# Where the block sums of the output weights are made, and how many buffers the block sums of h land in, in an encoder layer on one core

## The chip, the cores and the metric

The kernel runs on one core of one Trainium2 chip. The metric is the device time of one execution in microseconds (us); lower is better. Times before: 1134.73, 1137.67 and 1137.10 us, median 1137.1. The profile comes from a further execution.

The engines named below: TensorE (PE) multiplies matrices and leaves the sums in PSUM, which has eight banks here; VectorE (DVE) and GpSimd (POOL) do elementwise work, ScalarE (ACT) copies and evaluates functions, and SyncE (SP) issues every DMA of this kernel, in one queue and in order. An instruction that waits holds up all that stands behind it on its engine.

## The reference

One encoder layer is applied to two inputs with the same weights: a prompt of 512 tokens and a sample of 1024, each token with 1024 channels. Cut to what matters:

```python
h = rmsnorm(x, norm_g)
qa, ka, va, za, qb, kb, vb, zb, ga, gb = split(h @ w_in)
oa = (neighbourhood_attention(qa, ka, va, rpb_a) * silu(za)) @ w_o_a
ob = (window_gqa_attention(qb, kb, vb, t5_table, sink_b) * silu(zb)) @ w_o_b
merged = sigmoid(ga) * oa + sigmoid(gb) * ob
return x + merged @ w_out
```

All of it is 32-bit arithmetic.

## The kernel before, in words

**Products in three matmuls.** A 32-bit operand is split into a part `hi` that TensorE's fast 32-bit format holds exactly and a rest `lo` (`split`, L1170 on ScalarE for hi, L1175 on VectorE or GpSimd for lo). A product of two operands is then hi x hi, hi x lo and lo x hi (L1288, L1289, L1290). Weights go into `whi` and `wlo`, six buffers each; a chunk of h or of another moving operand is `hh` and `hl`. Each product of a 512x128 weight block with 512 columns is 12 matmuls.

**The stages.** For the prompt: attention, then the dense phase (`dense_phase`) with a z stage (silu gates), a gate stage, the merge (the two output products of the branches times their gates) and the output stage (`merged @ w_out` plus x). Then the same for the sample. In the profile the prompt's output stage lies from 351 to 394 us, the sample's attention from 394 to about 786, its z stage from 786, its output stage from about 1040 to the end.

**Seven products for eight.** The prompt's dense stages use plain products (`pair_classic`, `CLASSIC_P = (4, 8, 4)`): a pair of output chunks takes four raw weight blocks of 128x512, named (chunk m, half j). The sample's dense stages use Strassen's form in Winograd's variant: a pair takes seven products of half the size instead of eight. For it four sums of the raw weight blocks are needed (s1 = (1,0) + (1,1), s2 = s1 - (0,0), s3 = (0,0) - (1,0), s4 = (0,1) - s2), and four block sums of the moving operand, which `stored_sums` loads from DRAM (`t_d` for h, written long before; `m_d` for the merged values), block by block into buffers `U` (four), and splits into tiles `T`. Two of the seven products, and two of the weights, need no sum of h: (0,0) and (1,0) go with blocks of h; so does the seventh, s4 with the block (1,1) of h. The other four products use T.

**The z stage of the sample.** Ahead of the pairs, one product for each pair that needs only h is left in `fr` or `fl` (`kept_z`), and a second is added to it. `pair_strassen` then makes the remaining five products of each pair: three with T into running sums, the fourth with T, and last the one on h with s4.

**The output stage of the sample.** `pairs_apart` works in two rounds over four pairs. The first makes the products that need no T, the second the four others. The first round loads four raw blocks a pair, makes s1 to s4 on VectorE or GpSimd, and stores s1, s2 and s3 to `s_d` in DRAM (L1430); the second round loads them back (L1452) beside one raw block.

**What sets the order.** A planner (`Flow.run`) simulates the engines with costs for each operation and writes out one order for each engine before the kernel is built. Each operation has a priority number, lower first; among the operations that are ready an engine takes the lowest. Buffers of a tag are a ring: those of `IN_TURN` (`raw`, `whi`, `wlo`, `U`, `T`, `S`, `C`, `ot`, `w32`) are taken strictly in turn. A buffer is free when all operations that hold it have ended, DMAs included. `raw` has four buffers (`load_raw`, L1250 to 1253). On the chip the order of each engine is fixed; semaphores carry the real waits.

**Between the prompt and the sample** the pools of the prompt are closed when their last user has ended (`f.stage`), and the sample's mask and bias tables are then loaded. The attention weights (`att_weights`, L600 loads into `w32`, L602 and L607 split) follow the output weights in the same `whi` and `wlo` rings.

## Time and profile before

| what | before |
|---|---|
| median of three runs | 1137.1 us |
| profiled execution, its own time | 1136.88 us |
| its span, first to last instruction | 1135.1 us |
| TensorE busy | 1121.6 us, 99% of the span, 6079 matmuls |
| VectorE, ScalarE, GpSimd busy | 863.8, 653.7, 327.1 us |
| bytes moved by DMA | 186.11 MB, 164 GB/s mean |
| granted TensorE clock | 1.000 |

A row of a timeline gives the start in us from the span's first instruction, the duration in us, engine, line, operation, output tile, inputs, shapes and count; in brackets stands the idle time of that engine just before, and what ended it. Matmuls are pipelined, so their durations overlap: the distance from one start to the next tells the pace. A row of windows gives the stretch, its length, and for each of TensorE's matmuls, TensorE's weight loads, VectorE, ScalarE and GpSimd the busy time and the number of instructions, then the granted clock, the share of the DMA engines and GB/s. A row of the chain of waits gives a start, a duration and what the time went to.

Here is how many matmuls TensorE began in the stretches around the changed places; at full pace with 512 columns a stretch of 20 us has 90:

```profile
780.00:800.00 20.00, 20.00 (x94) 16.55 (x93) 12.30 (x23) 13.04 (x24) 0.00 (x0) 1.00 0.77 229
800.00:820.00 20.00, 19.31 (x82) 14.90 (x81) 16.78 (x28) 10.14 (x19) 0.47 (x1) 1.00 0.93 309
820.00:840.00 20.00, 19.57 (x86) 15.86 (x86) 19.09 (x27) 9.56 (x20) 8.68 (x8) 1.00 0.48 155
840.00:860.00 20.00, 20.00 (x90) 16.56 (x89) 17.36 (x26) 5.59 (x12) 5.93 (x5) 1.00 0.80 242
```

### The profile page before, as it was taken

What the parts mean: (1) busy time and instruction counts of PE and PEld (TensorE: products, weight loads), DVE (VectorE), ACT (ScalarE), POOL (GpSimd) and SP (SyncE); (2) the same over time, 40 slices, a digit from 0 to 9 for tenths busy, and PEclk for the clock granted to TensorE, in tenths of its full rate; (3) what the DMA queues carried; (4) which work ended last, traced back from release to release, by engine and by line L of the source; (5) the groups of instructions that cost most, each with busy time, mean ns of one, the idle gap of its engine ahead of it and who ended that gap; (6) DMA issues with size and microseconds to landing.
All of it is one profiled execution on the core that took longest, in us unless ns stands there. A gap on an engine that the chain in (4) does not pass through costs nothing.

```text
span 1135.1 us, 18686 instructions
## 1 busy us (share of the span) xinstructions
PE 1121.6 (99%) x6079; PEld 973.9 (86%) x6079; DVE 863.8 (76%) x1995; ACT 653.7 (58%) x1498; POOL 327.1 (29%) x432
## 2 busy tenths in 40 slices
PE   8999999999999999999999999999999999999998
PEld 6999988888888889999899988988788888788887
DVE  5888797587765468887868888885888866779874
ACT  6777987644433246574759888876534434522440
POOL 4654433000010044433414344420033221124221
PEclk9999999999999999999999999999999999999999
DMA  7854533488786422121312314244958645868982
GB/s 261 273 157 139 183 115 103 110 262 260 241 276 196 159 91 72 29 79 29 91 32 84 82 38 112 57 131 127 300 187 244 218 167 180 297 219 281 302 279 93
DMA packets 139108, 186.11 MB, mean 164 GB/s; under 512 B 29897, under 2 KB 68561, under 8 KB 139010
## 3 DMA queue, kind: packets, MB, share of 16 engines
q1 hardware_dynamic: 139010, 184.91, 51.4%
q8 instruction: 48, 0.79, 0.3%
q14 instruction: 50, 0.41, 0.1%
HBM read 138.71 MB, written 50.88 MB: 167 GB/s over the span
## 4 chain that ended last, share of the span: by engine, by line
PE 89%; DMA 4%; DVE 4%; ACT 1%; issue 1%; SPq 0%; POOL 0%; DVEq 0%; POOLq 0%; ACTq 0%
PE p L761 25%; PE x L1288 8%; PE x L1290 8%; PE x L1289 8%; PE x L1063 5%; PE x L1026 5%; PE x L934 5%; PE d L1288 4%; PE d L1289 4%; PE d L1290 4%; PE p L1289 4%; PE p L1290 4%; PE p L1288 4%; PE x L861 2%; DMA ot<-u_d 1%
## 5 line engine op out<-in xcount | busy, mean ns | idle before, releaser
L761 PE MATMUL p<-whi,hh 128*128 128x384 f32 x384 | 133.6, 348 | 0.0
L761 PE MATMUL p<-whi,hl 128*128 128x384 f32 x384 | 132.4, 345 | 0.0
L761 PE MATMUL p<-wlo,hh 128*128 128x384 f32 x384 | 132.2, 344 | 0.0
L978 ACT ACTIVATE sb<-sb,mx 128x384 f32<-128x384 f32 (+1 forms) x192 | 107.7, 565 | 22.9 <-DVE mx L969 22.6
L1170 ACT ACTIVATE whi<-raw 128x512 fp32r<-128x512 f32 (+1 forms) x136 | 79.4, 599 | 67.4 <-PE x L1289 46.3
L1289 PE MATMUL x<-T,whi 128*128 128x512 f32 x284 | 110.7, 390 | 0.3 <-DVE T L1175 0.2
L1288 PE MATMUL x<-T,whi 128*128 128x512 f32 x284 | 110.6, 390 | 0.0
L1290 PE MATMUL x<-T,wlo 128*128 128x512 f32 x284 | 110.5, 389 | 0.0
L761 PE MATMUL p<-whi,hb 128*128 128x384 f32 x384 | 107.8, 346 | 0.0
L1037 DVE TENSOR_TENSOR pp<-x,pp 128x512 fp32r<-128x512 f32 (+1 forms) x136 | 82.6, 639 | 20.3 <-ACT pp L1032 19.2
L1175 DVE TENSOR_TENSOR wlo<-raw,whi 128x512 fp32r<-128x512 f32 (+1 forms) x109 | 73.3, 682 | 26.5 <-ACT whi L1170 26.0
L1175 POOL TENSOR_TENSOR wlo<-raw,whi 128x512 fp32r<-128x512 f32 (+1 forms) x27 | 32.1, 1199 | 172.9 <-ACT whi L1170 160.2
L799 POOL TENSOR_TENSOR rs_r<-rs_v,mhalf 128x4 f32<-128x4 f32 (+1 forms) x72 | 79.9, 1109 | 5.7
L1032 ACT ACTIVATE pp<-x 128x512 fp32r<-128x512 f32 (+1 forms) x136 | 70.9, 561 | 18.2 <-PE x L1026 17.1
L792 POOL TENSOR_SCALAR rs_v<-ss 128x4 f32<-128x4 f32 (+1 forms) x72 | 26.0, 361 | 185.1 <-DVE ss L785 181.7
L1063 PE MATMUL x<-pp,v 128*128 128x256 f32 (+1 forms) x368 | 76.6, 322 | 0.0
L1288 PE MATMUL x<-hh,whi 128*128 128x512 f32 x196 | 76.4, 390 | 0.1
L1290 PE MATMUL x<-hh,wlo 128*128 128x512 f32 x196 | 76.3, 389 | 0.0
L1289 PE MATMUL x<-hl,whi 128*128 128x512 f32 x196 | 76.2, 389 | 0.0
L761 PEld LDWEIGHTS p<-whi,hl 128*128 128x128 f32 x384 | 72.8, 190 | 1.3 <-issue 1.0
L761 PEld LDWEIGHTS p<-whi,hh 128*128 128x128 f32 x384 | 73.0, 190 | 1.1 <-issue 0.5
L761 PEld LDWEIGHTS p<-wlo,hh 128*128 128x128 f32 x384 | 72.9, 190 | 0.9 <-issue 0.5
(381 smaller groups left out, 3011.9 us busy)
## 6 DMA issues: line engine op xcount, KB each, us to landing
raw<-in_w_g_dram SPq DMA_DIRECT2D x84, 256.0 KB
w<-in_w_att_dram SPq DMA_DIRECT2D x46, 384.0 KB
raw<-in_w_z_dram SPq DMA_DIRECT2D x40, 256.0 KB
ot<-o_d SPq DMA_DIRECT2D x36, 256.0 KB
raw<-in_w_out_dram SPq DMA_DIRECT2D x36, 256.0 KB
g_d<-C SPq DMA_DIRECT2D x34, 256.0 KB
fr<-in_w_g_dram SPq DMA_DIRECT2D x28, 256.0 KB
out_dram<-C SPq DMA_DIRECT2D x19, 256.0 KB
```

The costliest lines, as they stand in the source:

```text
L761: pe.matmul(ps.t[:, :GW], part[u](k), mv.t[:, c], start=k == 0 and m == 0, stop=k == KC - 1 and m == 2,)
L799: lambda e: nc.gpsimd.tensor_tensor(r.t[:, :nn], rv.t[:, :nn], mhalf[:, :nn], op=ALU.pow),
L934: pe.matmul(pss[2 * pair + i].t[:, :width], q.t[rows, u, at : at + P], kv[:, tiles[0] : tiles[-1] + 1 : step], start=n == 0, stop=n == 2,)
L978: act.activation(sb.t[:, :width], sb.t[:, :width], AF.Exp, bias=mx.t[:, i : i + 1], scale=-1.0, accum_out=sm.t[:, i : i + 1],)
L1032: lambda e, pt=pt, pp=pp, nn=nn: act.activation(pp.t[:, 0, :nn], pt.t[:, :nn], AF.Copy),
L1037: lambda e, pt=pt, pp=pp, nn=nn: dve.tensor_tensor(pp.t[:, 1, :nn], pt.t[:, :nn], pp.t[:, 0, :nn].bitcast(F32), op=ALU.subtract),
L1063: pe.matmul(out(), v.t[:, vs], mv(), start=first, stop=last)
L1170: (("act", ACT_(n)),), lambda e: act.activation(hi(), src(), AF.Copy), prio,
L1175: lambda e: engines[e].tensor_tensor(lo(), src(), hi().bitcast(F32), op=ALU.subtract), prio,
L1288: pe.matmul(out, hi.t[:, cs], mh(), start=first and k == 0, stop=False, **more)
L1289: pe.matmul(out, hi.t[:, cs], ml(), start=False, stop=False, **more)
L1290: pe.matmul(out, lo.t[:, cs], mh(), start=False, stop=last and k == len(ws) - 1, **more)
```

## The change

Three things are changed.

1. In the prompt's output stage `pair_classic` calls the new `weight_sums` for each pair: once both chunks' raw blocks have been split, the four sums are made in place in the raw buffers, one after the other, and all four are stored to `s_d`, which is now one tile for the whole kernel. In the sample's output stage `pairs_apart` makes no sums any more: the first round loads two raw blocks and s4, the second s1, s2, s3 and one raw block as before.
2. `stored_sums` for h lands every second block in `fh` or `w32` (two buffers each) instead of `U`, so that eight blocks can be under way; all these loads wait for the stage's opening.
3. In the first pair of the sample's z stage the product with s4 on h is issued before the products with T, and its PSUM bank is kept until its result is added at the pair's end.

```diff
@@ -403,6 +403,9 @@
     t_d = dpool.tile([4, 4, P, NT_S // 2], F32, tag="t_d", name="t_d")
     o_d = {geo.nt: dpool.tile([2, 8, P, geo.nt], F32, tag=f"o_d{geo.nt}", name=f"o_d{geo.nt}") for geo in (gp, gs)}
 
+    s_d = dpool.tile([4, 4, P, 512], F32, tag="s_d", name="s_d")
+    s_saves = {}
+
     def expand(geo, h, lo):
 
         run = 3 * geo.cw * 16
@@ -1147,7 +1150,6 @@
         g_d = dpool.tile([2, 8, P, nt], F32, tag=f"g_d{nt}", name=f"g_d{nt}")
         p_d = None if short else dpool.tile([2, 4, P, sn], F32, tag="p_d", name="p_d")
         m_d = None if short else dpool.tile([4, 4, P, sn], F32, tag="m_d", name="m_d")
-        s_d = None if short else dpool.tile([8, 3, P, nh], F32, tag="s_d", name="s_d")
         stores = {}
         h_reads = []
         tags = iter(ROTA * 50)
@@ -1228,6 +1230,9 @@
 
             return moving_sums(tv, ops)
 
+        def spare(tag):
+            return f.value(wpool, [P, nh], F32, tag, {"fc": 1}.get(tag, 2))
+
         def stored_sums(prio, d, after):
 
             tv, ops = {}, {}
@@ -1235,13 +1240,13 @@
                 tv[j] = tuple(f.value(tp, [P, 4, nh], F32R, "T", 8) for _ in range(2))
                 vh, vl = tv[j]
                 for k in range(4):
-                    st = tile_("U", 4)
+                    st = spare(("fh", "w32")[k // 2]) if not short and d is t_d and k % 2 else tile_("U", 4)
                     dma(
-                        lambda st=st, j=j, k=k: nc.sync.dma_start(st.t, d[j, k]), 512 * nh, prio, new=[st],
-                        after=after(j, k),
+                        lambda st=st, j=j, k=k: nc.sync.dma_start(st.t[:, :nh], d[j, k]), 512 * nh, prio, new=[st],
+                        after=[*after(j, k), *([opened] if d is t_d else [])],
                     )
                     ops[j, k] = split(
-                        lambda vh=vh, k=k: vh.t[:, k], lambda vl=vl, k=k: vl.t[:, k], lambda st=st: st.t, nh, prio,
+                        lambda vh=vh, k=k: vh.t[:, k], lambda vl=vl, k=k: vl.t[:, k], lambda st=st: st.t[:, :nh], nh, prio,
                         (vh, k == 0), (vl, k == 0), [st],
                     )
             return moving_sums(tv, ops)
@@ -1309,11 +1314,31 @@
 
             return mov
 
-        def pair_classic(srcs, post, prio, mov_h, after=lambda i: ()):
+        def weight_sums(i, raw, ends, prio):
+            o = None
+            for j, out, in0, in1, op in (
+                (2, (1, 1), (1, 0), (1, 1), ALU.add), (1, (1, 0), (0, 0), (1, 0), ALU.subtract),
+                (0, (0, 0), (1, 1), (0, 0), ALU.subtract), (3, (0, 1), (0, 1), (0, 0), ALU.subtract),
+            ):
+                v, a, b = raw[out], raw[in0], raw[in1]
+                o = tt(
+                    lambda v=v: v.t, lambda a=a: a.t, lambda b=b: b.t, op, 512, prio, hold=[v, a, b],
+                    after=[*ends, *([o] if o else [])],
+                )
+                s_saves[i, j] = dma(
+                    lambda v=v, j=j: nc.sync.dma_start(s_d[i, j], v.t), 262144, prio, after=[o], hold=[v],
+                )
+
+        def pair_classic(srcs, post, prio, mov_h, after=lambda i: (), sums_of=None):
 
             i = 0
+            raws, ends = {}, []
             for m, src in enumerate(srcs):
-                ws = weight_tiles([load_raw(src[j], prio - 2) for j in range(2)], 4, prio)
+                raws.update({(m, j): load_raw(src[j], prio - 2) for j in range(2)})
+                ws = weight_tiles([raws[m, j] for j in range(2)], 4, prio)
+                ends += [x for w in ws for *_, ops in w for x in ops]
+                if m and sums_of is not None:
+                    weight_sums(sums_of, raws, ends, prio + 0.5)
                 for n in halves:
                     ps = bank(next(tags))
                     o = product(ps, ws[0], mov_h(0, n), prio, True, False, after(i))
@@ -1368,6 +1393,7 @@
                     (("act", ACT_(sn)),), lambda e: act.activation(p1.t, a.t[:, :sn], AF.Copy), prio, new=[p1], use=[a]
                 )
                 result(0, 0, p1, mul(1, mov_h(1, 0)))
+            ps7 = mul(6, mov_h(1, 1)) if here and not prio else None
             add(u2, p1, mul(2, mov_t(1)))
             add(u3, u2, mul(3, mov_t(2)))
             b = mul(4, mov_t(0))
@@ -1375,7 +1401,7 @@
             result(1, 1, u3, b)
             result(1, 0, u3, mul(5, mov_t(3)), ALU.subtract)
             if not last:
-                result(0, 1, u4, mul(6, mov_h(1, 1)))
+                result(0, 1, u4, ps7 or mul(6, mov_h(1, 1)))
                 return
 
             c = seed(0, sn, sn, u4, prio)
@@ -1395,12 +1421,14 @@
                 post(0, nh + s.start, nh // 2, c, False, prio, s.start, [last_op])
 
 
-        def spare(tag):
-            return f.value(wpool, [P, nh], F32, tag, {"fc": 1}.get(tag, 2))
-
         def pairs_apart(jobs, prio, mov_h, mov_t, late, seed=None, ready=()):
 
             kept = []
+
+            def load_sum(i, j, prio):
+                v = tile_("raw", 4, 512)
+                dma(lambda: nc.sync.dma_start(v.t, s_d[i, j]), 262144, prio - 2, new=[v], after=[s_saves[i, j], start])
+                return v
 
             def take(ps, w, mov, pr, first, last, after=(), again=False, n=sn):
                 o = product(ps, w, mov, pr, first, last, [*after, *ready], n, again)
@@ -1412,24 +1440,9 @@
                     (("act", ACT_(sn, False)),), lambda e: act.activation(out.t, ps.t[:, :sn], AF.Copy), pr, new=[out], use=[ps],
                 )
 
-            for i, (at, srcs, post) in enumerate(jobs):
+            for i, (srcs, post) in enumerate(jobs):
                 pr = prio + i / 8
-                raw = {(m, j): load_raw(srcs[m][j], pr - 2) for m, j in ((0, 0), (1, 0), (1, 1), (0, 1))}
-                s1, s2, s4, s3 = (tile_("S", 3, 512) for _ in range(4))
-                saves = []
-                for j, out, in0, in1, op in (
-                    (2, s1, raw[1, 0], raw[1, 1], ALU.add), (0, s2, s1, raw[0, 0], ALU.subtract),
-                    (None, s4, raw[0, 1], s2, ALU.subtract), (1, s3, raw[0, 0], raw[1, 0], ALU.subtract),
-                ):
-                    tt(
-                        lambda out=out: out.t, lambda in0=in0: in0.t, lambda in1=in1: in1.t, op, 512,
-                        pr - 0.5 + (j == 1), new=[out], use=[in0, in1],
-                    )
-                    if j is not None:
-                        saves.append(dma(
-                            lambda j=j, out=out, at=at: nc.sync.dma_start(s_d[at, j], out.t), 262144, pr, use=[out],
-                        ))
-                w = weight_tiles([raw[0, 0], raw[0, 1], s4], 6, pr - 0.5)
+                w = weight_tiles([load_raw(srcs[0][0], pr - 2), load_raw(srcs[0][1], pr - 2), load_sum(i, 3, pr)], 6, pr - 0.5)
                 p1, c = (spare(t) for t in (("fr", "fl"), ("fr", "fl"), ("fh", "fc"), ("fh", "w32"))[i])
                 ps, p7 = bank(next(tags)), bank(next(tags))
                 take(ps, w[0], mov_h(0, 0), pr, True, True)
@@ -1442,16 +1455,11 @@
                     leave(c, p7, pr)
                 take(ps, w[1], mov_h(1, 0), pr, False, True, [o], True)
                 post(0, 0, sn, ps, True, pr)
-                kept.append((p1, c, saves))
-
-            for i, ((at, srcs, post), (p1, c, saves)) in enumerate(zip(jobs, kept)):
+                kept.append((p1, c))
+
+            for i, ((srcs, post), (p1, c)) in enumerate(zip(jobs, kept)):
                 pr = late + i
-                raw = []
-                for j in range(3):
-                    v = tile_("raw", 4, 512)
-                    dma(lambda v=v, j=j, at=at: nc.sync.dma_start(v.t, s_d[at, j]), 262144, pr - 2, new=[v], after=saves)
-                    raw.append(v)
-                w = weight_tiles([*raw, load_raw(srcs[1][1], pr - 2)], 6, pr - 0.5)
+                w = weight_tiles([*(load_sum(i, j, pr) for j in range(3)), load_raw(srcs[1][1], pr - 2)], 6, pr - 0.5)
                 pv = lambda v: (lambda: v.t[:, :sn])
 
                 def mul(j, t):
@@ -1744,7 +1752,7 @@
         mov_h = blocks(m_ops, nh)
         if not short:
             jobs = [
-                (4 + i, [[w_out[c, j] for j in range(2)] for c in (2 * i, 2 * i + 1)], lambda m, *a, i=i: post_out(2 * i + m, *a))
+                ([[w_out[c, j] for j in range(2)] for c in (2 * i, 2 * i + 1)], lambda m, *a, i=i: post_out(2 * i + m, *a))
                 for i in range(4)
             ]
             seeds = lambda i: lambda m, *a: with_x(2 * i + m, *a)
@@ -1755,7 +1763,7 @@
             srcs = [[w_out[c, j] for j in range(2)] for c in (2 * i, 2 * i + 1)]
             post = lambda m, *a, i=i: post_out(2 * i + m, *a)
             if i < o_classic:
-                pair_classic(srcs, post, 20 + i, mov_h)
+                pair_classic(srcs, post, 20 + i, mov_h, sums_of=i)
             else:
                 seed = lambda m, *a, i=i: with_x(2 * i + m, *a)
                 pair_strassen(srcs, post, 20 + i, mov_h, mov_t, seed, i == 3)
```

## The prediction, made before the change was run

> **What bounds the kernel now.** I read the page's shares first, then the count of matmuls in short windows, then TensorE's own rows where a window holds too few, and last the chain of waits behind each of these places.
>
> ```profile
> PE 1121.6 (99%) x6079; PEld 973.9 (86%) x6079; DVE 863.8 (76%) x1995; ACT 653.7 (58%) x1498; POOL 327.1 (29%) x432
> ```
>
> TensorE is busy for 1121.6 of 1135.1 us, and the change takes no matmul away. So it can only win back places where TensorE's rows stand apart. In the dense stages a 512-column matmul starts 0.227 us after the one before it; what a step has beyond that is lost. In the z stage of the sample (786 to 826 us) the wide steps are these:
>
> ```profile
> 811.13 0.50 PE L1288 MATMUL x<-T,whi 128*128 128x512 f32 x1
> 811.85 0.50 PE L1289 MATMUL x<-T,whi 128*128 128x512 f32 x1 [0.22 <-DVE T L1175]
> 812.19 0.39 PE L1290 MATMUL x<-T,wlo 128*128 128x512 f32 x1
> ...
> 814.50 0.39 PE L1288 MATMUL x<-T,whi 128*128 128x512 f32 x1
> 815.00 0.50 PE L1289 MATMUL x<-T,whi 128*128 128x512 f32 x1
> ...
> 818.99 0.39 PE L1288 MATMUL d<-T,whi 128*128 128x512 f32 x1
> 819.73 0.50 PE L1289 MATMUL d<-T,whi 128*128 128x512 f32 x1 [0.35 <-DVE T L1175]
> ...
> 822.35 0.39 PE L1288 MATMUL d<-T,whi 128*128 128x512 f32 x1
> 823.17 0.50 PE L1289 MATMUL d<-T,whi 128*128 128x512 f32 x1 [0.43 <-DVE T L1175]
> ```
>
> The steps are 0.72, 0.50, 0.74 and 0.82 us, so 2.78 less 4 x 0.227, which is 1.87 us. The step after a wait is 0.34 (811.85 to 812.19), 0.11 too long, four times: **2.3 us** in all. Each time a part of T, the split block sums of h, comes late. Why it does is in the SP queue and in ScalarE:
>
> ```profile
> 789.12 1.37 SPq L1240 DMA_DIRECT2D U<-t_d  x3
> ...
> 794.26 3.45 SPq L1512 DMA_DIRECT2D u_d<-C  x1
> ...
> 805.76 3.11 SPq L1240 DMA_DIRECT2D U<-t_d  x4
> ...
> 811.83 3.47 SPq L1240 DMA_DIRECT2D U<-t_d  x4
> ```
> ```profile
> 810.44 1.25 ACT L1170 ACTIVATE T<-U 128x512 fp32r<-128x512 f32 x2 [3.48 <-DMA U<-t_d]
> ...
> 818.12 2.55 ACT L1170 ACTIVATE T<-U 128x512 fp32r<-128x512 f32 x4 [3.59 <-DMA U<-t_d]
> ```
>
> Sixteen blocks land through four buffers U, in four waves. A wave's issue waits until the wave before it has been split, and the second also stands behind a store that holds the SP queue for 3.45 us. ScalarE waits over 3 us for each of the last two waves.
>
> In the sample's output stage (1040 to 1135) two steps are wide, 0.45 and 0.49 us:
>
> ```profile
> 1059.40 0.39 PE L1288 MATMUL p<-hh,whi 128*128 128x512 f32 x1
> 1059.85 0.50 PE L1289 MATMUL p<-hl,whi 128*128 128x512 f32 x1
> ...
> 1076.53 0.39 PE L1290 MATMUL x<-hh,wlo 128*128 128x512 f32 x1
> 1077.02 0.50 PE L1288 MATMUL x<-hh,whi 128*128 128x512 f32 x1
> ```
> ```profile
> 1059.12 0.68 DVE L1175 TENSOR_TENSOR hl<-fl,hh 128x512 fp32r<-128x512 f32 x1
> ```
> ```profile
> 1063.20 5.90 DMA s_d<-S
> 1069.12 5.38 DMA raw<-s_d
> ...
> 1074.60 0.64 ACT whi L1170 x2
> ```
>
> With the 0.11 behind each that is (0.45 + 0.49) - 2 x 0.227 + 0.22 = **0.7 us**. The first ends 0.05 us after VectorE has written hl; the second hangs on a store of weight sums, on their reload, and on the split of what was loaded.
>
> **The change part by part.**
>
> Eight landing buffers. The loads are the same sixteen; eight can be out at once, so the first eight are issued from 789 on, ahead of the store at 794.26, and the second eight as those are split. The last wave then is issued where 805.76 stands instead of 811.83, about 6 us earlier, against lateness of 2.3 us in all. fh and w32, which lend the four new buffers, were last read in the fill of the gates and by the attention, before this stage. The cover could fail if the DMA engines are full anyway:
>
> ```profile
> 796.00:800.00 4.00, 4.00 (x20) 3.30 (x19) 3.70 (x8) 2.32 (x6) 0.00 (x0) 1.00 1.15 349
> ...
> 824.00:828.00 4.00, 4.00 (x19) 3.32 (x18) 3.96 (x8) 3.05 (x7) 1.74 (x2) 1.00 0.00 0
> ```
>
> They are at their limit near 796 and idle at 824 (the last two columns are their share and GB/s): work is there to be pulled forward, but not all of it.
>
> The product on h ahead. These are the same 12 matmuls, 12 x 0.227 = 2.7 us, run before the first pair's T products instead of behind them. Every T product is then wanted up to 2.7 us later. That alone is more than 2.3. Its weights are the last sum of the pair, made long before 809. It holds one of the eight PSUM banks for a pair; I cost that at nothing, because VectorE empties the other seven within the 2.7 us of a product (if not, a product waits for a bank, some 0.7 us, one eviction as in the DVE row above). Value taken for both edits: -2.3; bounds -2.4 and 0, the latter if the burst of eight delays the stage's weights by as much as it saves.
>
> Output stage of the sample. It loses 16 sums, 12 stores and 4 loads of 256 KB (three raw loads a pair instead of four, no s_d store). A sum costs VectorE 0.68 as in the DVE row, so some 11 us of work go, and no reload waits for a store any more. Both causes of the 0.7 lie in this work. Taken: -0.6; bounds -0.9 and 0.
>
> Output stage of the prompt. It gains the same 16 sums and 16 stores. Work as such is hidden:
>
> ```profile
> 345.00:380.00 35.00, 35.00 (x156) 28.98 (x155) 16.86 (x26) 9.76 (x16) 1.12 (x1) 1.00 0.52 170
> ```
>
> VectorE has 18 of 35 us free and takes 16 x 0.68 = 11 in 43 us; the DMA share of 0.52 takes 16 x 0.26 MB more, 4.2 MB in 43 us or about 100 GB/s on 170. What is not hidden by that is the ring: the four raw buffers are now held until a pair's sums are made in place and stored. Before, a raw was free when its split ended and its next load went out at once. Now the loads of pair i+1 wait for: all eight splits of pair i, three sums, a store, and only then a load and a split. The times of this stage:
>
> ```profile
> 348.53 0.69 DVE L1175 TENSOR_TENSOR wlo<-raw,whi 128x512 fp32r<-128x512 f32 x1 [1.44 <-ACT whi L1170]
> ...
> 362.00 0.69 DVE L1164 TENSOR_TENSOR C<-x,C 128x512 f32<-128x512 f32 x1 [1.54 <-PE x L1290]
> ...
> 367.43 0.69 DVE L1164 TENSOR_TENSOR C<-x,C 128x512 f32<-128x512 f32 x1 [1.54 <-PE x L1290]
> ```
> ```profile
> 334.72 0.33 SPq L1721 DMA_DIRECT2D ot<-g_d  x1
> ...
> 362.71 0.34 SPq L1575 DMA_DIRECT2D out_dram<-C  x1
> ...
> 364.72 0.33 SPq L1561 DMA_DIRECT2D C<-in_xt_p_dram  x1
> ```
> ```profile
> 337.77 0.63 ACT L1505 ACTIVATE ot<-ot 128x512 f32<-128x512 f32 x1 [1.89 <-DMA ot<-g_d]
> ```
>
> A chunk of the output takes TensorE 5.43 us (362.00 to 367.43), a pair 10.9. A store takes 2.0 us until its buffer is loaded again (362.71 to 364.72, the SP queue waits for just that), a load 3.05 (334.72 to 337.77), together 5.1. A split takes ScalarE 0.63 and VectorE 0.69, 1.3. Pair 0's last split ends at 349.2; VectorE still has the merge to do there, so I put the end of its third sum at 353.6, twice the 2.1 us that three sums take alone. Pair 1's first weights are ready at 353.6 + 5.1 + 1.3 = 360.0, and are needed when chunk 1 ends, at 361.9: 1.9 to spare. From then on a round costs 2.1 (three sums) + 5.1 + 1.3 + 2.1 (three more splits) + 0.7 (one output sum between them) = 11.3 against 10.9, so 1.5 and 1.1 are left at pairs 2 and 3. With store and load together x, the lateness at pair 3 is 3(x - 5.1) - 1.1. It is positive from x = 5.5. Bounds: 0 at this stage's 5.1, and at 6.3, a middle value for a queue that is fuller, 2.5. Taken: +0.4, since the stage stays below full.
>
> The passage into the sample's attention. The whi ring is used in turn, so late splits of the output weights push the first attention weights back, and the SP queue with them. The chain there:
>
> ```profile
> 391.69 0.86 ACT whi L602
> ...
> 393.93 3.90 DMA fr<-in_w_g_dram
> ...
> 400.94 4.73 DMA mask<-in_mask_s_dram
> 405.96 0.71 POOL bias L695
> ```
>
> By the round above the last w_out split falls some 3 us later than now. If the order of the SP queue stays, the mask lands 3 us later, and GpSimd's normalising step, which stands behind the bias, with it. The loads may also be ordered anew, which could do away with the wait. Bounds -1.2 and +3; taken: +0.2.
>
> **The sum**: -2.3 - 0.6 + 0.4 + 0.2 = -2.3 us. The profiled execution took 1136.9 (span 1135.1), and the median of the three runs is 1137.1, 0.2 above it. So 1134.6 against the execution, and **1134.8** as a median.
>
> **The rivals.**
>
> Burst only. The eight loads move in front of weights that are then late, or the product ahead finds its weights late: the z stage keeps 1.5 of its 2.3. For it speaks the share above 1 at 796, against it the idle queue at 824. Time 1134.8 + 1.5 = 1136.3; within 0.3% of before.
>
> More stalls go. The order of everything behind 350 us is worked out anew, and two stalls that the change doesn't aim at may shrink, the 1.2 us before 408 and the 1.0 us of the window 540 to 560:
>
> ```profile
> 400.00:420.00 20.00, 18.84 (x114) 17.53 (x114) 13.34 (x43) 7.83 (x20) 9.22 (x14) 1.00 0.30 89
> ...
> 540.00:560.00 20.00, 19.00 (x126) 17.42 (x125) 16.70 (x47) 13.38 (x36) 9.80 (x10) 1.00 0.36 113
> ```
>
> That would be 1134.8 - 2.0 = 1132.8. Against it: nothing in the diff removes their causes.
>
> The held raws stall TensorE (slower than before). One mechanism, the ring of four in the prompt's output stage. If store and load take what they take in the sample's output stage, 5.9 and 5.4 by the chain, x is 11.3; halfway from 5.1 to there, at 8.2, the formula gives 3 x 3.1 - 1.1 = 8.2, and the time is 1134.8 - 0.4 + 8.2 = 1142.6. Slower than before it is from a loss of 2.9, so from x = 6.4. For it speaks that every reload hangs on a write; against it that the DMA share is 0.52 here and that this stage's own store took 2.0.
>
> The Trainium skill (HBM Reference, Latency) speaks for this rival: it gives an access 0.2 us on average and 2 us at high load. By that figure, as an estimate, store and load would each grow by up to 1.8, x would be 8.7, and the time 1144.1. The two stages agree in direction: a 256 KB store took 2.0 us here and up to 5.9 in the sample's output stage.
>
> **How the numbers follow.** Runs of this kernel differ by up to 0.26%, so 0.3%, 3.4 us, is what can be told from no change: faster means below 1133.7, slower above 1140.5. The forecast has 0.55, with a range of its own from 1133.3 to 1136.2; burst only 0.15; more stalls go 0.15; the held raws 0.15. Faster: most of the third case and a fifth of the forecast, 0.24. Slower: the worse two thirds of the last case, and a little of the passage, 0.12. Within: 0.64. The range from 1132.2 to 1138.8 holds the forecast, the burst and nearly all of the third case, with the milder half of the last.
>
> **What would show it.** Steps of 0.227 throughout 809 to 824, U, fh and w32 loaded from t_d within some 15 us of the opening, and one h product between T products there, would bear out the z stage. No s_d store behind 400 us and no wide step near 1060 and 1077 would bear out the output stage. The raws of pairs 1 to 3 should be issued right behind an s_d store, with TensorE's steps at 0.227 from 362 to 394; wide steps at 372 and 383 there would show the ring as the loss. A wait over 1.2 us before the first transposes of the sample's attention would show the passage. The forecast is wrong if TensorE's rows in 786 to 826 keep their gaps, or if it stands for over 2.5 us in 350 to 410.

## The result and the profile after

The changed kernel takes 1138.27 us (median of 13 runs, 1135.13 to 1140.51); the kernel before, run beside it, 1135.46. The ratio of the two is 1.0021, with a 95% interval from 1.0013 to 1.0030: about 2.4 us slower, where 2.3 us faster had been forecast. The profiled execution took 1139.11 us (span 1137.3), 2.2 above the 1136.88 of before.

TensorE's work is the same (6079 matmuls, 1121.3 us busy), and the splits of raw weights on ScalarE now wait first of all for loads (the page's group of these splits: busy time, mean of one, idle time ahead of them and what ended it). Before, the largest releaser of the splits was TensorE (46.3 us), which had yet to free the ring.

```profile
L1172 ACT ACTIVATE whi<-raw 128x512 fp32r<-128x512 f32 (+1 forms) x140 | 81.3, 600 | 70.2 <-DMA raw<-in_w_out_dram 23.5
```

Where the time went is told by TensorE's busy time and count in the same stretches of both kernels (window, its length, then busy time and count of PE, PEld, DVE, ACT and POOL, the granted clock, DMA share and GB/s). First the kernel before, then the changed one:

```profile
394.00:430.00 36.00, 34.55 (x213) 32.14 (x212) 24.09 (x70) 16.84 (x42) 15.24 (x23) 1.00 0.33 102
...
530.00:580.00 50.00, 49.00 (x324) 45.74 (x322) 37.93 (x115) 31.86 (x88) 18.92 (x23) 1.00 0.23 66
...
786.00:826.00 40.00, 38.88 (x167) 30.72 (x166) 32.05 (x52) 22.62 (x42) 2.59 (x2) 1.00 0.82 263
...
1050.00:1090.00 40.00, 39.84 (x175) 32.34 (x174) 32.40 (x51) 21.12 (x39) 8.93 (x7) 1.00 0.93 321
```
```profile
394.00:430.00 36.00, 32.56 (x193) 30.36 (x193) 22.41 (x60) 16.73 (x39) 14.43 (x23) 1.00 0.46 149
...
530.00:580.00 50.00, 50.00 (x338) 47.09 (x337) 38.73 (x113) 31.39 (x87) 15.56 (x24) 1.00 0.21 62
...
786.00:826.00 40.00, 38.53 (x169) 31.20 (x168) 33.70 (x50) 22.61 (x43) 9.37 (x6) 1.00 0.87 270
...
1050.00:1090.00 40.00, 40.00 (x178) 33.02 (x177) 26.93 (x42) 18.69 (x36) 9.40 (x8) 1.00 0.84 277
```

The passage into the sample's attention (394 to 430) stands idle for 3.44 us instead of 1.45. The 1.0 us near 550 is gone. The z stage (786 to 826) does 169 matmuls instead of 167, two steps of 0.227, where ten were looked for. The sample's output stage does 178 instead of 175: its 0.7 us is won.

The prompt's output stage itself, from its first dense matmul to the first of the sample's attention, grew from 43.52 to 44.64 us. Two places make this up: 0.38 near 357 and 0.65 near 385. The first is seen in VectorE's rows of the changed kernel and, behind them, in ScalarE's last split of the merge's result, before and after:

```profile
350.46 1.47 DVE L1166 TENSOR_TENSOR raw<-raw 128x512 f32<-128x512 f32 x2
...
353.72 0.69 DVE L1166 TENSOR_TENSOR raw<-raw 128x512 f32<-128x512 f32 x1 [0.59 <-POOL raw L1166]
354.33 0.68 DVE L1166 TENSOR_TENSOR ot<-p,ot 128x512 f32<-128x512 f32 x1
355.05 0.69 DVE L1166 TENSOR_TENSOR C<-C,ot 128x512 f32<-128x512 f32 x1
```
```profile
353.04 0.63 ACT L1170 ACTIVATE hh<-C 128x512 fp32r<-128x512 f32 x1 [1.47 <-DVE C L1164]
...
355.77 0.63 ACT L1172 ACTIVATE hh<-C 128x512 fp32r<-128x512 f32 x1 [4.56 <-DVE C L1166]
```

Three of pair 0's sums (raw<-raw) stand in VectorE's order in front of the merge's last steps (ot<-p,ot and C<-C,ot), and the third waits for the one that GpSimd makes. The last split of the merge's result, hh, then starts at 355.77; before it was 353.04. In both kernels the gates' last step on ScalarE, which the merge needs, had started shortly before (347.35 and 348.06), so the split falls 7.7 us behind it instead of 5.7.

The second is the ring of raw buffers. ScalarE's splits of the last output weights, first before, then changed, and then in e10 (a kernel of the experiments, with the same holds around short sums and stores):

```profile
378.09 0.63 ACT L1170 ACTIVATE whi<-raw 128x512 fp32r<-128x512 f32 x1 [2.09 <-PE x L1289]
...
384.58 0.63 ACT L1172 ACTIVATE whi<-raw 128x512 fp32r<-128x512 f32 x1 [8.65 <-DMA raw<-in_w_out_dram]
387.06 1.26 ACT L1172 ACTIVATE whi<-raw 128x512 fp32r<-128x512 f32 x2 [0.43 <-DMA raw<-in_w_out_dram]
...
380.22 1.26 ACT L1172 ACTIVATE whi<-raw 128x512 fp32r<-128x512 f32 x2 [0.67 <-DMA raw<-in_w_out_dram]
```

In the changed kernel the first split of pair 3 waits for its load, and TensorE's first product of pair 3 (385.26) follows it. The last of these splits ends at 388.3 instead of 378.7.

In the z stage the loads of t_d did not all go out ahead of the store. SP queue of the changed kernel:

```profile
792.11 0.42 SPq L1245 DMA_DIRECT2D U<-t_d  x1
792.57 0.43 SPq L1245 DMA_DIRECT2D fh<-t_d  x1
793.05 0.43 SPq L1245 DMA_DIRECT2D U<-t_d  x1
793.58 0.85 SPq L1257 DMA_DIRECT2D raw<-in_w_z_dram  x2
794.47 0.43 SPq L1245 DMA_DIRECT2D w<-t_d  x1
...
797.52 3.62 SPq L1520 DMA_DIRECT2D u_d<-C  x1
...
801.72 0.40 SPq L1245 DMA_DIRECT2D U<-t_d  x1
```

Four are out, then weights, loads of ot and two stores take their place, and the fifth is issued at 801.72.

### The profile page after: what moved, and what is told of

It reads as the page before. It is cut to its first block, busy times and chain, and to the rows that moved or that the text cites. A ratio compares the mean times of both kernels' runs of the same rounds, so it can differ in the third digit from the quotient of the medians.

```text
span 1137.3 us, 18702 instructions
## 1 busy us (share of the span) xinstructions
PE 1121.3 (99%) x6079; PEld 973.9 (86%) x6079; DVE 861.5 (76%) x1990; ACT 652.4 (57%) x1499; POOL 335.4 (29%) x436
## 4 chain that ended last, share of the span: by engine, by line
PE 88%; DMA 5%; DVE 3%; issue 2%; ACT 1%; POOL 1%; SPq 0%; POOLq 0%; ACTq 0%; DVEq 0%
PE p L764 25%; PE x L1294 8%; PE x L1293 8%; PE x L1295 8%; PE x L1066 5%; PE x L937 5%; PE x L1029 5%; PE d L1293 4%; PE p L1294 4%; PE d L1295 4%; PE p L1295 4%; PE d L1294 4%; PE p L1293 4%; PE x L864 2%; DMA raw<-in_w_out_dram 1%
## 5 line engine op out<-in xcount | busy, mean ns | idle before, releaser
L1294 PE MATMUL x<-T,whi 128*128 128x512 f32 x280 | 108.9, 389 | 0.0
L1293 PE MATMUL x<-T,whi 128*128 128x512 f32 x280 | 108.9, 389 | 0.0
L1177 DVE TENSOR_TENSOR wlo<-raw,whi 128x512 fp32r<-128x512 f32 (+1 forms) x111 | 75.7, 693 | 34.3 <-ACT whi L1172 31.8
L1177 POOL TENSOR_TENSOR wlo<-raw,whi 128x512 fp32r<-128x512 f32 (+1 forms) x29 | 35.1, 1219 | 198.6 <-DMA raw<-in_w_g_dram 111.9
L764 PEld LDWEIGHTS p<-whi,hb 128*128 128x128 f32 x384 | 69.1, 188 | 3.0 <-issue 1.3
```

The source lines that it names most:

```text
L764: pe.matmul(ps.t[:, :GW], part[u](k), mv.t[:, c], start=k == 0 and m == 0, stop=k == KC - 1 and m == 2,)
L1177: lambda e: engines[e].tensor_tensor(lo(), src(), hi().bitcast(F32), op=ALU.subtract), prio,
L1293: pe.matmul(out, hi.t[:, cs], mh(), start=first and k == 0, stop=False, **more)
L1294: pe.matmul(out, hi.t[:, cs], ml(), start=False, stop=False, **more)
```

## The experiments

**How to read the table.** Ratios are against the kernel before, run on the same chip. The stage columns come from one profiled execution of each kernel. "Prompt's output" is the time from the first dense matmul of that stage (the first on hh) to the first matmul of the sample's attention, as the difference to before (350.92 to 394.44, 43.52 us). "Last gate" says how long ahead of that first dense matmul ScalarE started the last gate's step (ot<-ot). "Passage" is the time from the first matmul of the sample's attention to its first transposes, as the difference to before (394.44 to 403.04, 8.60 us). "Idle" is how long TensorE stands in the first 36 us of the sample's attention. The last column counts the executions whose mean granted clock was 1.00 to three places; of the kernel before, 81 of 94 were.

| kernel | ratio, 95% interval | prompt's output | last gate | passage | idle | at full clock |
|---|---|---|---|---|---|---|
| before | 1 | 0 | 3.57 | 0 | 1.45 | 81 of 94 |
| changed kernel | 1.0021 [1.0013, 1.0030] | +1.1 | 3.85 | +3.8 | 3.44 | 9 of 13 |
| e1 sums alone | 1.0034 [1.0023, 1.0045] | +4.0 | 1.85 | +3.1 | 1.32 | 5 of 12 |
| e2 z part alone | 1.0009 [0.9993, 1.0024] | 0.0 | 4.06 | +0.4 | 0.74 | 9 of 12 |
| e3 sums in own buffers, no wait for splits | 1.0059 [1.0039, 1.0080] | +5.2 | -0.24 | +0.5 | 0.92 | 1 of 6 |
| e4 z part, loads first | 0.9981 [0.9969, 0.9992] | +0.6 | 1.51 | -0.1 | 0.31 | 11 of 12 |
| e5 sums in own buffers, after the merge | 1.0060 [1.0044, 1.0076] | +5.5 | 0.15 | +3.4 | 5.02 | 0 of 6 |
| e6 sums in place, after the merge | 1.0111 [1.0094, 1.0129] | +3.4 | 4.51 | +1.4 | 1.17 | 0 of 6 |
| e7 landing buffers, loads first, nothing else | 0.9978 [0.9967, 0.9989] | +0.2 | 1.91 | +0.5 | 0.86 | 12 of 12 |
| e8 is e5 and e4 together | 1.0047 [1.0033, 1.0061] | +0.9 | 3.97 | +3.2 | 3.92 | 1 of 6 |
| e9 (rows: e13) work, no hold | 1.0052 [1.0033, 1.0070] | +4.2 | 1.25 | +0.2 | 0.90 | 0 of 7 |
| e10 hold, hardly any work | 1.0041 [1.0024, 1.0059] | 0.0 | 4.01 | +2.7 | 3.11 | 3 of 12 |
| e11 sums of pairs 0 and 1 | 1.0010 [0.9992, 1.0029] | +2.2 | 2.30 | +0.5 | 0.83 | 5 of 12 |
| e12 whole change, loads first | 0.9984 [0.9967, 1.0002] | +2.0 | 3.55 | +3.4 | 1.97 | 8 of 12 |
| e14 added sums, no stores | 1.0074 [1.0062, 1.0086] | +2.1 | 2.08 | -0.3 | 0.58 | 0 of 5 |
| e15 added stores, no sums | 0.9998 [0.9988, 1.0007] | 0.0 | 2.91 | -0.1 | 0.33 | 9 of 11 |
| e16 sums of pairs 0 to 2 | 1.0070 [1.0056, 1.0084] | +3.0 | 2.88 | +1.4 | 0.80 | 4 of 6 |

**What a single profile can tell.** The changed kernel, e1 and e12 issue the same instructions in the same order on every engine until 785 us, and yet their prompt's output stages grew by 1.1, 4.0 and 2.0 us; e5 and e8, which also agree until the z stage, by 5.5 and 0.9. What differs is when the last gate came: 3.85, 1.85 and 3.55 us ahead in the first three, 0.15 and 3.97 in the other two. The loads of g_d, which the gates wait for, run later against TensorE in one profile than in another; why wasn't tested. e2, e4 and e7, which agree with before until 788, differ by 2.5 us in this, too. What an edit does to the merge is seen better from the last gate to the start of the last split of hh: 7.6 to 7.8 us wherever whole sums stand ahead of the merge's end behind the splits (the changed kernel, e1, e11 to e14, e16), 5.5 to 6.2 where none does (before, e2, e4 to e8, e10, e15), and 6.6 in e3, whose sums stand earlier. So sums there delay the merge by about 2 us in every one of these kernels. TensorE waits for what the split starts later than about 3.5 us behind the stage's first dense matmul: 0.4 us at 3.9 (the changed kernel), 0.7 at 4.2 (e12), 1.4 at 4.8 (e16), 1.9 at 5.4 (e11), 2.4 at 5.9 (e1). In the profile before it started at 2.1.

The measured ratio lies above every range that was written down for e3, e6, e8, e9, e14 and e16, and by a hair for e1 and e10; for e2 and e11 it lies between the two ranges given.

**Which part costs: e1 and e2.** e1 is the changed kernel with the z part taken out (cut; the loads' wait for the stage's opening goes too):

```diff
-                    st = spare(("fh", "w32")[k // 2]) if not short and d is t_d and k % 2 else tile_("U", 4)
+                    st = tile_("U", 4)
-            ps7 = mul(6, mov_h(1, 1)) if here and not prio else None
-                result(0, 1, u4, ps7 or mul(6, mov_h(1, 1)))
+                result(0, 1, u4, mul(6, mov_h(1, 1)))
```

> Part 1 of the change alone: the sums of output weights move to the prompt's output stage; the z stage is as before. Ring theory: the raw buffers, held until the sums are stored, make the splits of the output weights late, and these push back the attention weights; so TensorE shows about 1 us of wide steps between 350 and 390 us and 2 to 3 us more before the transposes near 408, and wins back 0.7 us at the end of the sample; time 1.001 to 1.003 of before. Rival, the loss comes from the z stage: no loss in 350 to 420 beyond 0.5 us, time 0.999 to 1.000 of before.

e2 is the kernel before with just these lines as the changed kernel has them:

> Parts 2 and 3 alone: eight landing buffers and the product on h ahead; the sums of output weights are made and stored in the sample's output stage as before. Ring theory: the matmuls up to 780 us start as before (within 0.3 us), the z stage wins 0.5 us and no more, since the second four blocks stand behind a store in the SP queue; time 0.999 to 1.0005 of before. Rival, the z stage costs: time 1.001 to 1.003 of before, with a wide step of over 1 us near 815.

The sums alone cost 3.9 us (1.0034). The z part alone gains nothing that can be told (1.0009). So the loss is the first part's, and the z part does not pay as it is written. In the z stage the changed kernel wins 0.4 us, but so does the profile of e1, which has no z part.

**Why the z part does not pay: e4 and e7.** In e4 the loads of t_d come ahead of everything else in the planner's order; e7 is e4 without the product ahead.

```diff
-                        lambda st=st, j=j, k=k: nc.sync.dma_start(st.t[:, :nh], d[j, k]), 512 * nh, prio, new=[st],
+                        lambda st=st, j=j, k=k: nc.sync.dma_start(st.t[:, :nh], d[j, k]), 512 * nh, prio - 4 * (d is t_d), new=[st],
```

> Parts 2 and 3 alone, and the loads of h's block sums go ahead of every other load of the z stage in the SP queue. If the prediction's mechanism holds (the blocks come late because they wait for buffers and for the queue), eight loads are out before the first u_d store, T is split before it is wanted, and the wide steps of 809 to 824 go: 2.0 to 2.3 us, 0.998 of before. Rival, the DMA engines are the bound there: the weights or the blocks of o_d are late in their turn, TensorE shows gaps of 1 us or more elsewhere between 790 and 830, time 0.9995 to 1.002 of before.

> Eight landing buffers with their loads ahead of all others, without the product on h ahead. If early loads are what closes the gaps: 0.998 to 0.9985 of before, as with the product ahead. If the product ahead does it: wide steps of 1 us or more are left at 809 to 824, 0.999 to 1.000.

Both are faster, and by as much: 0.9981 and 0.9978. The SP queue of e7, and its window:

```profile
788.11 0.43 SPq L1243 DMA_DIRECT2D U<-t_d  x1
...
791.43 0.43 SPq L1243 DMA_DIRECT2D w<-t_d  x1
...
792.50 0.53 SPq L1512 DMA_DIRECT2D u_d<-C  x1
```
```profile
786.00:826.00 40.00, 40.00 (x178) 33.09 (x178) 35.54 (x55) 24.66 (x48) 10.68 (x9) 1.00 0.88 285
```

Eight loads are out by 791.9, the store of u_d is issued behind them and holds the queue for 0.53 us instead of 3.45, and the stage does 178 matmuls instead of 167: eleven steps of 0.227, 2.5 us, the gain of the whole kernel. e7 has no product ahead, so this gain is that of the landing buffers with their loads first. Whether the loads' place alone would do it, with four buffers, wasn't tested. e7 has the lowest ratio of this study.

**Do the parts add up: e12 and e8.** e12 is the changed kernel with the line of e4; e8 is e5 (below) with e4's lines.

> The whole change, and the loads of the z stage's block sums ahead of every other transfer in the planner's order. If the parts add up, it is the change's ratio less the 2.2 to 2.5 us that the loads first gave beside the kernel before: 1.0021 - 0.0021, so 0.9985 to 1.0010, with no wide step in 809 to 824 and 2 to 4 us lost by the first transposes of the sample's attention. If the change of order reaches back into the prompt's output stage (the order of everything behind 350 us is worked out as one), the loss there is another one, and the ratio is above 1.0020.

> The whole change with both mendings: sums into buffers of their own after the merge, and the loads of h's block sums first. The gains add: 2.3 us in the z stage and up to 0.7 in the sample's output stage, 0.9975 to 0.9985 of before. If the sums' move still costs: 0.9985 to 1.001.

e12 comes to 0.9984, and its window from 786 to 826 has 178 matmuls as in e7. The parts add up there: 1.0021 less the z gain is 0.9999, inside its interval. e8 is 0.13% below e5, with overlapping intervals; its profile wins the 2.5 us in the z stage too.

**Where the sums should stand: e3, e5, e6.** Three tries to rescue the first part. In e3 (the rest as in the changed kernel) the sums go to buffers of their own and wait for no split; in e5 (without the z part) they also wait until the merge is split; in e6 (without the z part too) they stay in place and wait for the merge.

```diff
-                v, a, b = raw[out], raw[in0], raw[in1]
-                o = tt(... hold=[v, a, b], after=[*ends, *([o] if o else [])],
-                )
+                v, a, b = spare(tag), raw[in0], raw[in1]
+                tt(... new=[v], use=[a, b])
+                raw[out] = v
```
```diff
+                tt(... new=[v], use=[a, b], after=[x for ops in m_ops.values() for x in ops])
```
```diff
-                    after=[*ends, *([o] if o else [])],
+                    after=[*ends, *(x for ops in m_ops.values() for x in ops), *([o] if o else [])],
```

> The whole change, but the four sums of a pair go into buffers of their own (fr, fl, fh, which nothing else uses in that stage) instead of back into the raw ones, so a raw buffer is free when it has been read and not when the store has landed; sums, stores and loads are as many. Ring theory: the output weights are split at TensorE's pace again, the last one near 378 us and not 387, there are no wide steps in 350 to 390 and the passage costs no more than before; time 0.998 to 0.9995 of before. Rival, the added stores, sums or the new order as such cost: 1.001 to 1.003 of before, as the change itself.

> Part 1 alone, sums into buffers of their own, and none of them before the merge of the prompt has ended. Theory now: two things cost, the sums that stand in VectorE's queue in front of the merge's last split (4 us in the run of part 1 alone), and the raw buffers held until the stores have landed (the passage). Both are taken away here, so the matmuls of the prompt's output stage take 43.5 us as before, within 0.7, the first transposes come within 1 us of before against the start of the attention, and the time is 0.999 to 1.0005 of before. Rival, the sixteen added stores and sums cost wherever they stand: 1.002 or more.

> Part 1 alone, sums in place in the raw buffers as in the change, none before the merge has ended. By the theory the merge's last split is as early as before, so there is no stall at the first output chunk, but the ring is held longer: stalls of 1 to 3 us at the second or third pair and 2 to 4 us in the passage; 1.002 to 1.005 of before. If only the merge's split counted: 0.9995 to 1.0005.

All three are worse than the sums alone. e5 was to show that the merge's place and the hold explain the loss, and e5 and e8 do clear the merge: its last split falls 5.8 us behind the last gate, as without sums. e5's 5.5 us in this stage come mostly from a last gate that was late in its profile and from the half pace behind it, and e8, with the same order there, loses 0.9. But the hold isn't gone in them: the raw buffers wait for sums that wait for the merge, the loads and stores then leave together (one reload in e5's chain of waits took 6.92 us), and the last splits of the output weights start at 389.4 and 386.5 (378.1 before). In the passage e5 and e8 stand idle for 5.0 and 3.9 us. e6 shows the ring alone: the merge is clear of sums, and its 3.4 us are waits for splits of late raw buffers, 1.2 at pair 1 (362.9) and 2.1 at pair 3 (386.9). Another 4.5 of its 9.5 us are lost in the z stage (below).

**Work or hold: e9, e13 and e10.** e9 adds the work without the hold: sums of other data into buffers of their own, and stores to a place that nobody reads. The outputs stay as they are. Its profiled execution took 3944 us and is left out, so its rows are those of e13, the same kernel.

```diff
+        def side_work(i, raw, ends, prio):
+            o = None
+            for j, tag in enumerate(("fr", "fl", "fh", "fr")):
+                v = f.value(wpool, [P, nh], F32, tag, 2)
+                o = tt(... hh.t[:, j] ... hl.t[:, j] ..., ALU.add, 512, prio, new=[v], hold=[hh, hl], after=[*ends, *([o] if o else [])])
+                dma(lambda v=v, j=j: nc.sync.dma_start(q_d[i, j], v.t), 262144, prio, use=[v])
```

> The kernel before, with the work of the first part added to the prompt's output stage, but without its hold: behind the splits of each pair, VectorE or GpSimd makes four sums of 512 columns from hh and hl into buffers of their own (fr, fl, fh, fr), and each is stored, 256 KB, to a place that nobody reads. The four raw buffers come free as before, and the sample's output stage makes its own sums as before. Theory 'hold' (what costs is that a raw buffer waits for sums and store before its next load goes out): the raw loads go out as before, the last split of w_out stays near 378 us, the passage into the sample's attention stays within 0.7 us of before, ratio 0.9990 to 1.0010. Theory 'work' (what costs is 16 more sums in VectorE's order ahead of the merge, and 4.2 MB of stores): the step behind the merge is late as in the sums alone, ratio 1.0020 to 1.0045.

> The kernel with the added work and no hold once more, for its rows. If VectorE's order is what costs, the two last steps of the prompt's merge (ot<-p,ot and C<-C,ot, near 351 and 352 us before) stand behind one or more of the added sums, and the step from the T products to the first product on hh is over 1 us wide with hh or hl as releaser; behind it the granted clock is below 1 for some 4 us. If the stores are what costs, that step is as before (0.23 to 0.40 us), and the wide steps have a DMA as their source.

e10 is the counterpart: the change's own chain of sums and stores with its holds, on 32 of the 512 columns.

```diff
+                o = tt(lambda v=v: v.t[:, :32], lambda a=a: a.t[:, :32], lambda b=b: b.t[:, :32], op, 32, prio, hold=[v, a, b], after=[*ends, *([o] if o else [])])
+                dma(lambda v=v, j=j: nc.sync.dma_start(q_d[i, j, :, :32], v.t[:, :32]), 16384, prio, after=[o], hold=[v])
```

> The counterpart: the same chain of sums in place and stores, with the same holds on the four raw buffers, but on 32 of the 512 columns only, so that the work is a sixteenth; the sample's output stage makes its own sums as before, whole. Theory 'hold': the last split of w_out comes at 385 us or later, TensorE stands 0.4 to 1 us near 385, and the passage opens 2.5 to 4 us later than before; ratio 1.0020 to 1.0040. Theory 'work': as before, ratio 0.9990 to 1.0010, since sums and stores that short take nothing from VectorE or the DMA engines. A result between the two would say that the hold costs only with stores of full size behind it, since store and reload are then slower.

In these profiles the work costs 4.2 us in the prompt's output stage and nothing in the passage. The hold of e10 costs nothing in the prompt's output stage (43.52, as before) and 2.7 in the passage. But e10 doesn't hold the raw buffers as long as the change: its last split of output weights ends at 381.5, where the changed kernel's ends at 388.3 and 385 or later had been expected, and the stall near 385 did not come. So e10 clears a short hold in that stage, not the change's. Nor is its ratio of 1.0041 the price of the hold: of the 6.0 us in its profile, 4.0 are lost in the sample's output stage, where its lines are those of before and TensorE waits 1.93 us for hh at 1063.5, with half pace behind. In the passage it is the weights of the gates that come late in e10. The chain of waits:

```profile
397.10 4.80 DMA fr<-in_w_g_dram
401.92 0.64 ACT fh L1172
402.59 0.31 DVE fl L1177
...
403.97 1.28 POOL rs_r L801
405.28 0.43 DVE qk L818
```

VectorE works in order: the sums of squares for the first transposes stand behind the split fl, which waits for the load fr; GpSimd's normalising step follows. That load is issued 3.2 us later than before (393.93 there, and 3.90 long).

**Sums or stores: e14 and e15.** The two halves of e9 apart: e14 leaves out its stores; e15 stores hh as it is, without a sum.

```diff
-                dma(lambda v=v, j=j: nc.sync.dma_start(q_d[i, j], v.t), 262144, prio, use=[v])
```
```diff
+            for j in range(4):
+                dma(lambda j=j: nc.sync.dma_start(q_d[i, j], hh.t[:, j].bitcast(F32)), 262144, prio, after=ends, hold=[hh])
```

> The added sums alone: sixteen sums of 512 columns from hh and hl behind the splits of each pair, into buffers of their own, and no store. Raw buffers come free as before, and the sample's output stage makes and stores its own sums. If VectorE's order costs: ratio 1.0020 to 1.0050, with a step over 1 us wide at the prompt's first product on hh. If the stores cost: 0.9990 to 1.0010, since VectorE has 18 of 35 us free there.

> The added stores alone: behind the splits of each pair four stores of 256 KB, of hh as it is, to a place that nobody reads; no sum. If the stores cost (4.2 MB more in the SP queue and on the DMA engines, in front of the attention's weights): ratio 1.0015 to 1.0045, with the first transposes of the sample's attention over 1 us later than before. If VectorE's order costs: 0.9990 to 1.0010.

The stores cost nothing (0.9998), the sums alone 0.74%, most of it not where they stand (below). VectorE's rows of e14, and GpSimd's:

```profile
348.91 1.74 DVE L1166 TENSOR_TENSOR C<-C,ot 128x512 f32<-128x512 f32 x1
350.57 1.79 DVE L1177 TENSOR_TENSOR wlo<-raw,whi 128x512 fp32r<-128x512 f32 x1
352.28 0.68 DVE L1166 TENSOR_TENSOR fr<-hh,hl 128x512 f32<-128x512 f32 x1
...
354.69 0.68 DVE L1166 TENSOR_TENSOR fh<-hh,hl 128x512 f32<-128x512 f32 x1
355.29 0.68 DVE L1166 TENSOR_TENSOR ot<-p,ot 128x512 f32<-128x512 f32 x1
```
```profile
348.80 1.30 POOL L1166 TENSOR_TENSOR fl<-hh,hl 128x512 f32<-128x512 f32 x1
350.05 1.76 POOL L1166 TENSOR_TENSOR fr<-hh,hl 128x512 f32<-128x512 f32 x1
```

Two sums stand ahead of the merge's ot<-p,ot as in the changed kernel, and two of VectorE's own operations take 1.74 and 1.79 us instead of 0.69 while GpSimd makes the other two. TensorE then waits for hh, 1.3 us and some wide steps behind it, 2.1 in all; in e13 the last gate came 0.8 later, and half pace follows, which makes 4.2. The rest of e14's loss, 5.0 of 7.4 us, is far away, in the z stage, where the first loads of t_d go out at 799.25 (789.12 before):

```profile
806.33 0.49 PE L1290 MATMUL x<-T,whi 128*128 128x512 f32 x1 [3.04 <-ACT T L1172]
```

The same wait of 3.04 us stands in e6 and e13, and e16 waits there too (1.85). None of these kernels changes a line of the z stage: the order of everything behind 350 us is worked out as one, and in e14 the attention's last result (o_d) is stored at 796.83 us, where before it was 786.70, so the stage opens late. Why the order comes out so wasn't tested. So a total of this study is read only with its stages beside it, and e14's 0.74% is not the price of sixteen sums.

**How many pairs: e11 and e16.** The first part for pairs 0 and 1, and for pairs 0 to 2; the others are summed in the sample's output stage as before. Both are without the z part (cut; for e16 it is i < 3).

```diff
-                pair_classic(srcs, post, 20 + i, mov_h, sums_of=i)
+                pair_classic(srcs, post, 20 + i, mov_h, sums_of=i if i < 2 else None)
```

> The first part for pairs 0 and 1 alone: the sums of pairs 2 and 3 are made in the sample's output stage as before, and their raw buffers in the prompt's output stage come free as before. If the passage is late because the last output weights are late (pairs 2 and 3 catch up here, since a round has about 1 us to spare without the hold), it opens within 1 us of before, and the prompt's side costs at most 1 us; half of the 0.7 in the sample's output stage is won: ratio 0.9990 to 1.0008. If each sum costs where it is made, it is half of what the sums alone cost: ratio 1.0015 to 1.0025.

> The first part for pairs 0 to 2; pair 3 is summed in the sample's output stage as before. Its raw buffers still come late, by the hold of pair 2, but no store of pair 3 stands in the SP queue in front of the attention's weights. If these stores, which wait for their sums at the head of the queue, are what opens the passage late: it opens within 0.7 us of where the stage's own delay puts it (attention's weights loaded in the order of before, the mask 9.3 us behind the stage's end or less), ratio 1.0000 to 1.0020. If the late splits of the last output weights do it through the whi ring: 2 us or more later, ratio 1.0020 to 1.0040.

With two pairs the passage is as before (+0.5) and what is left is the place of pair 0's sums (+2.2). With three the transposes come 1.4 later, and with four 3.8 (3.1 in e1). Not all of that is lost: in the changed kernel, e1 and e12 nine more matmuls of 0.17 us each stand ahead of these transposes than before, in e6 and e16 three more, in e5 and e8 four fewer. TensorE stands no longer than before in the passage of e16 (0.80 us) and e1 (1.32). e1's stage ends 1.5 us later than the changed kernel's and its transposes come 0.8 later, so a TensorE that is late already has less to wait for, and the two columns don't add up. Whether the hold of pair 2, that of pair 3 or pair 3's stores delay the transposes is left open; e16's profiled execution is also 3.2 us faster than its median (1139.99 against 1143.20), so its rows don't hold all of its loss. Stores behind the last pair without a hold, in e13 and e15, do nothing to the passage.

## Why the prediction was wrong

**The z stage** (-2.3 forecast; about -0.4 in the changed kernel, and as much in e1 without a z part). This is the largest part of what was off. The cause of the stall and its size were right: with the loads first, 2.5 us come back. The step that failed is "the first eight are issued from 789 on, ahead of the store at 794.26". Eight free buffers allow that, but the order of the queue is the planner's, and it put weights, ot and u_d between. The bound of 0 was given for weights late by the burst; the cause was another one. The step "That alone is more than 2.3" about the product ahead isn't borne out: the changed kernel has it and waits 1.23 us for a T product, and e7 does without it. Of the two signs of being wrong that were written down, this one came: the gaps in 786 to 826 stayed.

```profile
816.34 0.50 PE L1294 MATMUL d<-T,whi 128*128 128x512 f32 x1 [1.23 <-DVE T L1177]
```

**The sample's output stage** (-0.6 forecast, -0.7 measured) came out right in the changed kernel's profile: its two wide steps are gone, and e15 shows beside it that a store as such costs nothing in the prompt's output stage. It isn't a safe gain: with the same lines there, e1's profile loses 1.2 us and e12's 0.5, by one wait near 1088 and 1085 (1.64 and 0.92 us) for ScalarE's fh, which stands in its order behind splits of late loads of m_d. The bracket "three raw loads a pair instead of four" is miscounted: raw loads fall from five to three a pair and loads of sums rise from three to four, which over four pairs still makes four loads fewer.

**The prompt's output stage** (+0.4 forecast; +1.1 in the changed kernel's profile). The +0.4 stood for the ring of raw buffers, and the ring was right: it costs 0.65 at the start of pair 3 in the changed kernel, 1.2 in e12, 1.5 in e16 and 3.4 in all in e6, in the bounds of 0 and 2.5 for all but e6. What the forecast put at nothing is the merge. "Work as such is hidden: VectorE has 18 of 35 us free" goes by a share over the whole stage; e14, without a hold or a store, shows that it isn't hidden in the 5 us in which the merge ends, where sums delay the last split by about 2 us. And "VectorE still has the merge to do there, so I put the end of its third sum at 353.6" let the sums wait for the merge, where the merge waits for the sums; the time itself was near (354.4). That only 0.4 of the 2.0 us reached TensorE in the changed kernel's profile is luck: its last gate came 3.85 us ahead of the stage, and in e1, with 1.85, the same order lost 2.4 us there and 1.6 more to half pace behind it.

**The passage** (+0.2 forecast of bounds -1.2 and +3). The mechanism was named rightly: late splits push the attention's weights back, and the mask behind them. Its sizes weren't: the last split of w_out ends 9.6 us later than before, where "some 3 us" was worked out, and the mask's load is issued 2.8 us later (400.94 to 403.76), of which 1.0 stood before the change did anything. The choice of a value near the middle was wrong. The chain of the changed kernel to the second transposes:

```profile
395.93 4.41 DMA w<-in_w_att_dram
...
400.44 0.86 ACT whi L605
...
403.76 5.30 DMA mask<-in_mask_s_dram
...
410.71 1.49 DVE bias L698 x5
```

TensorE stands 2.0 us more from 394 to 430. Half of this comes back near 550, where the 1.0 us that the rival "more stalls go" had named is gone; the other stall it named grew.

**The sum of the changed kernel's profile**: the stretch ahead of 350.92, where the change does nothing, ended 1.0 later; +1.1 prompt's output, +2.0 passage, -1.0 near 550, -0.4 z, -0.7 sample's output make 2.0, and a wide step near 973 is 0.4 wider. That is 2.4, against 2.2 measured between the two profiled executions.

**The clock.** The sum had no term for it. Behind some of its waits TensorE's matmuls run at half pace, and the granted clock in the records falls. e10, TensorE's rows and windows:

```profile
402.61 0.34 PE L763 MATMUL p<-whi,hl 128*128 128x384 f32 x1
405.76 0.48 PE L863 MATMUL x<-ident,qk 128*128 128x128 f32 x2 [2.81 <-DVE qk L818]
...
406.36 0.53 PE L763 MATMUL p<-wlo,hh 128*128 128x384 f32 x1
406.68 0.53 PE L763 MATMUL p<-whi,hl 128*128 128x384 f32 x1
...
409.69 0.33 PE L763 MATMUL p<-whi,hh 128*128 128x384 f32 x1
409.86 0.34 PE L763 MATMUL p<-wlo,hh 128*128 128x384 f32 x1
```
```profile
402.00:408.00 6.00, 3.19 (x15) 2.87 (x14) 4.12 (x11) 4.08 (x9) 2.08 (x4) 0.83 0.68 220
408.00:414.00 6.00, 6.00 (x33) 5.96 (x32) 3.21 (x12) 1.08 (x4) 2.99 (x6) 0.88 0.11 33
```

A wait of 2.8 us, then steps of 0.32 instead of 0.17 until 409.4: ten steps and 1.5 us on top. In e1 a wait of 1.61 is followed by 3 us of steps of 0.43 instead of 0.227, 1.6 us on top, with a granted clock of 0.88 from 354 to 360 and 0.83 from 360 to 366.

It does not follow every wait: the changed kernel's own, 1.78 us ahead of 408.92, has none behind it. So a kernel whose stalls are this long has executions with and without, and most of the kernels with long stalls in the table have few at full clock. It isn't the main cost of the changed kernel: its nine executions at full clock average 1137.75 us, those of before, taken beside the experiments, 1135.81, so about 1.9 of the loss stands without it.

## What to carry to other kernels

A buffer more lets a load go early, but the queue's order decides whether it does: look at what else may be issued in that time, and raise the load's place along with the buffer (here 0.9978 with both, 1.0009 with the buffers and the product ahead alone). Work moved to an engine that is half idle is hidden only if nothing urgent stands behind it in that engine's order; read the rows of the 5 us around the critical hand-over, not the share of the stage. When a whole program's order is worked out as one, judge an edit by its stages and not by the total. And before a stage's time in one profile is put down to an edit, look at two kernels with the same order there: here such pairs differed by up to 4.6 us.

## What the runs showed of the hardware that was not expected

Half pace after a wait much shorter than expected: waits of 1.45 us (e5, granted clock 0.78 from 354 to 360), 1.61 (e1) and 2.81 (e10) were followed by some 3 to 4 us of half pace, and waits of 1.64 (e1, near 1088), 1.78 (changed kernel) and 2.32 (e5, near 410) were not. The Trainium skill (TensorE: Matmul & The Clock Gate, Part 1) gives about 3.4 us as the window of idleness behind which the clock is halved, and calls the window free-running; half pace and the chance in it agree with these rows, the length doesn't.

VectorE and GpSimd can slow each other: in e14 two 512-column operations on VectorE took 1.74 and 1.79 us while GpSimd worked beside it, against 0.69 alone, and GpSimd's second sum 1.76 against 1.30 of its first. Not every operation is stretched: the two that VectorE began at 347.60 and 348.20, beside GpSimd's step before, took 0.68 each, and both read one operand from PSUM. Whether that is what spares them wasn't tested.

A load that left among four stores took 6.92 us (e5), where one by itself took 3.05; sixteen stores spread over the stage without sums cost nothing (e15).
